# A rewritten beginning, lighter first attention steps, and a halved second group of the first MLP in a hybrid encoder block

## The chip, the cores and the metric

The kernel runs on one core of a Trainium2 chip. The metric is the device time of the whole launch in microseconds (us). A core has a matrix engine (PE, with its weight loads listed apart as PEld), a vector engine (DVE), an activation engine (ACT), a general engine (GpSimd, POOL in the profile) and a sequencer that mainly issues transfers (SP). Each works through its own queue in program order, and waits for others by semaphores.

## The reference

```python
def reference(x, norm1_g, w_in, q_norm_g, k_norm_g, rpb, conv_w, w_attn_branch,
              w_conv_branch, w_o, norm2_g, w_mlp_in, w_mlp_out):
    ...
        u = rms_norm(x, norm1_g[l])
        proj = u @ w_in[l]
        q, k, v, cb, cc, ch, ga, gb = jnp.split(proj, split_pts, axis=-1)
        q = rms_norm(q.reshape(B, S, N_HEADS, HEAD_DIM), q_norm_g[l])
        k = rms_norm(k.reshape(B, S, N_HEADS, HEAD_DIM), k_norm_g[l])
        v = v.reshape(B, S, N_HEADS, HEAD_DIM)
        y_a = neighbourhood_attention(q, k, v, rpb[l]) @ w_attn_branch[l]
        y_b = short_gated_conv(cb, cc, ch, conv_w[l]) @ w_conv_branch[l]
        merged = jax.nn.sigmoid(ga) * y_a + jax.nn.sigmoid(gb) * y_b
        x = x + merged @ w_o[l]
        h = rms_norm(x, norm2_g[l]) @ w_mlp_in[l]
        x = x + jnp.square(jax.nn.relu(h)) @ w_mlp_out[l]
```

There is one layer. x has 1024 tokens of 1024 float32 values, q, k and v are 512 wide (8 heads of 64), the conv's three inputs 512 each, the gates 1024 each, and the MLP's hidden layer 4096. Attention is local on a grid of 16 x 64 tokens, with a relative-position bias.

## The kernel before

**Numbers.** Every float32 operand of a matmul is written as a sum of two float16 tensors, hi (the rounded value, written by ACT or GpSimd) and lo (what is left, written by DVE as `x * scale - hi`). A product then takes three matmuls, hi x hi, hi x lo and lo x hi (`PASSES`). Weight chunks are scaled by a power of two first, which is found from their largest value or their sum of squares: a reduction, a column `ones<-sc`, a matmul with ones (L201) that sums over the partitions, and a few 128x1 operations (`pow2`, `pow2_half`). The scaled chunk's hi pieces are made on ACT (L310), its lo pieces on DVE (L301).

**Tiling.** Tokens are cut into 8 rows of 128. An LN row b goes through the generator `norm`: a square with its sum (ACT L438), the reciprocal root `rstd` (one operation on ACT, five on DVE), the hi half u[b] (GpSimd for rows 1 to 3, ACT otherwise), and the lo half (DVE L446). Then u is transposed to uT: rows 0 to 2 by PE (`ln_trans`, 2 x 8 matmuls with an identity, copied out by ACT and DVE), rows 3 to 7 by a DMA on SP (`ln_turn`). A V unit is 24 matmuls (8 pieces of the inner dimension by three passes). V's weights come as two chunks of 256 columns: units of rows 0 to 2 run as halves (256 wide), those of rows 3 to 7 as one (512 wide). Then follow 8 Q units, 8 K units, and the conv's first chunk.

**Stages.** Begin and V, to 63.6 us; Q, to 105; K, to 148; conv's first part; then attention. In that stage each of the steps k = 0 to 79 issues a score matmul (`at_qk`), a softmax on DVE and ACT (`at_max` L845 is its first operation on DVE), a transposing DMA, and products with V (`at_pv`, L888), and between these `emit(n)` puts conv matmuls. A bias piece for the next quarter is formed in two operations (`bias_make`, DVE L606) at steps 9 and 11 of the 16. Then come the gates and branches, the output projection, and the first MLP from about 650 us. It works in groups (`quad(q)`) of seven products with sums between them; groups 0 and 1 are computed in halves of 256 columns, 0 low, 1 low, 0 high, 1 high. `h_done` then applies relu and square (ACT L1493, L1495), forms sums (L1215, DVE for groups 0 and 1, GpSimd after), and stores the group (`hs<-as`, SP L1506). Behind it comes the second MLP.

**Order.** Nothing is scheduled for the kernel: the order in which Python issues instructions is their order in each engine's queue. Work that runs beside the main line is written as generators: `step()` advances those of the list fg, `tick()` those of bg (weight chunks), `ln_step(b)` the LN row b; a unit's eviction (`post`) goes out after the next unit's matmuls.

`sforms` is one of the fg generators. For a later use (the gates' inputs) it scales pairs of LN rows in place (xt, ACT L499), lets GpSimd form sums and differences of them (L503), and writes these as hi and lo (ACT L508, DVE L510). Its steps are tied to a count of PE units, `SFORM`:

```python
    SFORM = ((6, 0, 0), (7, 1, 0), (8, 0, 1), (10, 2, 0), (10, 1, 1), (11, 3, 0), (14, 2, 1), (15, 3, 1))
        for mark, n, split in SFORM:
            yield from apart(mark, 0)
```

Here (6, 0, 0) is the scaling of rows 0 and 4 when six units are issued, (8, 0, 1) the hi and lo of their sums when eight are.

Of the kernel before, what the change touches and what calls it, by code (L numbers as in the profile page):

```python
# [10 lines left out]
F32 = mybir.dt.float32  # L11
# [41 lines left out]
def encoder_block(ctx: ExitStack, tc: tile.TileContext, x, weights, cols, gqk, rel, masks, out):  # L53
# [12 lines left out]
    def bank(tag):  # L66
        return psum.tile([128, 512], F32, name="ps_" + tag, tag=tag, bufs=banks[tag])
# [132 lines left out]
    def all_sum(a, out, bk, floor, lag=1):  # L200
        T.matmul(bk[:, 0:1], ones[:, 0:128], a, start=True, stop=True)  # L201
# [28 lines left out]
    def load_into(t, ch, p):  # L230
        m = ch.widths[p][0] * ch.widths[p][1]
        SP.dma_start(t, bass.AP(tensor=weights.tensor, offset=weights.offset + ch.offs[p], ap=[[m, 128], [1, m]]))

# [8 lines left out]
    class Chunk:  # L242


        def __init__(self, kind, widths, tag, rows, half, more):
            self.kind, self.bank = kind, {"V": "o", "Q": "o", "K": "s", "C": "d"}.get(kind)
            self.tag, self.rows, self.widths, self.more = tag, rows, widths, more
            self.offs = []
            self.raw, self.ready, self.half = [], more > 0, half
            self.split = False  # L250

        def prep(self):
# [4 lines left out]
            tot = sum(k * w for k, w in self.widths)  # L257
            if self.kind in "QKCG" or self.half:
                self.parts = vhome[0][:, 1] if self.half else wsp.tile([128, 2, tot], F16, name="w16_ws", tag="ws")
# [7 lines left out]
                V.tensor_reduce(sc[:, a], sc[:, at(rm, 0, n)], axis=AX, op=OP.add)  # L267
                c = ones_col()
                V.tensor_tensor(c, sc[:, a], sc[:, gm2], op=OP.mult)
                if self.half:  # L270
                    yield
                else:
                    yield from apart(units[0], 2 if self.kind == "Q" else 3)
                yield from all_sum(c, b, bank(self.bank) if self.bank else anybank(), 1e-36, not self.half)
# [8 lines left out]
            if self.half is not None:  # L283
                if not self.half:
                    vhome.append(wsp.tile([128, 2, 2, tot], F16, name="w16_v", tag="ws"))
                self.parts = vhome[0][:, self.half]
            elif self.kind not in "QKCG":
                self.parts = wpool[self.tag].tile([128, 2, tot], F16, name="w16_" + self.tag, tag=self.tag)
# [27 lines left out]
        def largest(self, rm, a, b):  # L316
# [15 lines left out]
            V.tensor_copy(c, sc[:, a])  # L332
            if self.kind != "V":
                yield from apart(units[0], 3 if self.kind != "O" else 1 + (self is cO[1]))
            yield from all_sum(c, b, bank(self.bank) if self.bank else anybank(), 1e-30, self.kind != "V")

# [97 lines left out]

    def norm(xin, sq, u, y, pool):
# [5 lines left out]
        if pool:  # L441
            G.tensor_scalar(u[:, 0], xin, sc[:, y], 1.0, op0=OP.mult, op1=OP.mult)
        else:
            A.activation(u[:, 0], xin, AF.Copy, scale=sc[:, y])
        yield
        V.scalar_tensor_tensor(u[:, 1], xin, sc[:, y], u[:, 0], op0=OP.mult, op1=OP.subtract)  # L446

    def ln_trans(u16, b, dst):
        for s in range(2):
            pt = bank16("o")  # L450
            for k in range(8):
                T.transpose(pt[:, k * 128:(k + 1) * 128], u16[:, s, k * 128:(k + 1) * 128], ident)
            o = dst[:, s, :, b * 128:(b + 1) * 128]
            i = pt.rearrange("p (k t) -> p k t", k=8)
            if s == 0:
                A.activation(o, i, AF.Copy)
            else:
                V.tensor_copy(o, i)

# [82 lines left out]
    push(cV[0])  # L542
# [8 lines left out]
    ln_step(1, 5)  # L551
    flush()
    v_unit(0, 0, 0, 0)
    ln_step(2)
    push(cV[1])
    tick()
    ln_step(2)
    tick()
    ln_step(1)
    ln_step(2, 5)  # L560
    tick()
    ln_trans(u16[:, 1], 1, UT)
    tick(7)
    v_unit(1, 0, 0, 0)
    ln_step(3)
    ln_step(2)
    tick()
    ln_trans(u16[:, 2], 2, UT)
    ln_step(3)
    tick()  # L570
    ln_step(3, 4)
    fg.append(qk_gain())
    fg.append(sforms())
    for p in range(11):
        if p == 3:
            flush()
            push(cQ)
        if p == 1:
            step()
            tick(2)  # L580
        elif p and p < 6:
            v_unit(p % 3, p // 3, 1, 2)
        elif p > 5:
            v_unit(p - 3, None, 0, 4 if p < 7 else 8)
        for q in (p,) if p < 6 else (2 * p - 6, 2 * p - 5):
            c = q // 2 + 3
            if c < 8 and q % 2 == 0:
                ln_step(c, 2)
                ln_turn(u16[:, c % 4], c, UT)
                turned[0] = c + 1  # L590
            if c < 7:
                ln_step(c + 1, 3)
        if p > 5:
            step(2)
    settle()
# [888 lines left out]
    c1w = c1  # L1484
    bsum, R = [keep(4 if i else 5) for i in range(4)], [(keep(), keep()) for _ in range(4)]
    r_ready = [False] * 4

    def h_done(q, c0=0, c1=512, wait1=0, wait2=0):
# [26 lines left out]
    def quad(q, c0=0, c1=512):  # L1515
# [295 lines left out]
```

## Time and profile before

| | |
|---|---|
| median of 3 runs | 1224.2 us (1222.97 to 1225.59) |
| the profiled execution | 1223.85 us |
| its span, first to last instruction | 1221.9 us |
| PE busy | 1194.5 us, 98%, 6294 matmuls |
| DVE, ACT, POOL busy | 933.2, 763.1, 428.7 us |

The profile is of one execution; its span lies 1.95 us below that execution's time. A row of the timeline has start, duration, engine, line of the kernel, operation, output <- input, shape and count, and in brackets the idle time before it with what ended it. Names are those of the program: w_v and w_ws are the hi and lo weights of V and of Q, K and conv, raw the weights as loaded, u and uT an LN row before and after its transpose, sc small columns of scales, ps_* banks of PSUM, s the forms made by `sforms`, vT the results of V.

### The profile page before, as it was taken

How to read it: one execution, taken by the hardware profiler on the slowest of the kernel's cores; microseconds unless marked ns; L12 is line 12 of the kernel's file. 1: busy time of each engine (PE TensorE's matmuls, PEld its weight loads, DVE VectorE, ACT ScalarE, POOL GpSimd, SP SyncE). 2: the span in 40 equal slices, each digit the busy share in tenths (PEclk: the TensorE clock that was granted, in tenths of full speed). 3: DMA queues.
4: the chain of work that ended last, by engine and by line, in shares of the span. 5: the costliest groups of instructions: out<-in, count | busy, mean ns of one | idle time of the engine just before them, and what ended most of it. 6: DMA issues, size and time to landing. Idle time of an engine off the chain costs nothing.

```text
span 1221.9 us, 17060 instructions
## 1 busy us (share of the span) xinstructions
PE 1194.5 (98%) x6294; PEld 572.8 (47%) x6294; DVE 933.2 (76%) x1754; ACT 763.1 (62%) x1183; POOL 428.7 (35%) x276
## 2 busy tenths in 40 slices
PE   5999999999999999999999999999999999999998
PEld 4544444554444444444458444444444444444444
DVE  6667879888368686887888666456447999998997
ACT  6776678878445455436668777687775754646440
POOL 1430003131321111101004476655658372563562
PEclk9999999999999999999999999999999999999999
DMA  7548556756542121226196455355374935435202
GB/s 278 108 183 180 111 127 123 152 113 131 127 123 61 44 69 40 65 67 244 21 178 173 164 190 163 130 181 175 129 274 164 348 125 183 162 121 207 104 35 104
DMA packets 170867, 173.35 MB, mean 142 GB/s; under 512 B 131488, under 2 KB 132000, under 8 KB 166688
## 3 DMA queue, kind: packets, MB, share of 16 engines
q1 hardware_dynamic: 170208, 168.07, 47.0%
q10 hardware_dynamic: 576, 4.19, 0.9%
q8 instruction: 49, 0.80, 0.3%
q14 instruction: 34, 0.28, 0.1%
HBM read 102.51 MB, written 37.75 MB: 115 GB/s over the span
## 4 chain that ended last, share of the span: by engine, by line
PE 69%; DVE 18%; ACT 7%; issue 4%; DMA 3%; SPq 0%; POOL 0%; ACTq 0%; DVEq 0%
PE ps_d L210 23%; PE ps_s L210 20%; PE ps_o L210 15%; PE ps_d L911 8%; DVE w_s L1033 2%; PE ps_o L888 1%; PE ps_s L831 1%; DVE ops L1644 1%; DMA qD<-q 1%; DVE w L1033 1%; DVE w_ws L301 1%; DVE s L510 1%; DVE sg L1149 1%; ACT w_ws L263 1%; DVE u L446 1%
## 5 line engine op out<-in xcount | busy, mean ns | idle before, releaser
L210 PEld LDWEIGHTS <-ops 128*128 128x128 f16 x1356 | 132.4, 98 | 159.4 <-issue 2.4
L210 PEld LDWEIGHTS <-w 128*128 128x128 f16 x1368 | 132.8, 98 | 141.9 <-issue 2.0
L911 PE MATMUL ps_d<-uT,w_ws 128*128 128x512 f16 x528 | 125.4, 379 | 0.0
L210 PE MATMUL ps_d<-ops 128*128 128x512 f16 (+1 forms) x528 | 118.3, 374 | 0.0
L210 PE MATMUL ps_s<-ops 128*128 128x512 f16 x492 | 113.2, 379 | 1.5 <-DVE sc L112 0.8
L1635 ACT ACTIVATE ops<-hf,sc 128x2048 f16<-128x2048 f32 x26 | 52.0, 1999 | 95.2 <-PE ps_o L210 35.7
L1022 POOL TENSOR_TENSOR tsum<-raw 128x512 f32<-128x512 f32 x28 | 47.2, 1701 | 142.6 <-ACT raw L1008 142.6
L210 PEld LDWEIGHTS <-uT 128*128 128x128 f16 x648 | 63.6, 99 | 68.5 <-issue 5.9
L1215 POOL TENSOR_TENSOR as<-as 128x512 f32<-128x512 f32 x56 | 77.8, 1389 | 43.1 <-ACT as L1495 39.8
L210 PEld LDWEIGHTS <-w_s 128*128 128x128 f16 x588 | 56.7, 98 | 69.5 <-DVE w_s L1033 1.9
L210 PE MATMUL ps_d<-u2x,w 128*128 128x512 f16 (+1 forms) x360 | 80.0, 372 | 0.0
L210 PE MATMUL ps_o<-ops 128*128 128x512 f16 x336 | 77.1, 379 | 0.0
L1637 DVE SCALAR_TENSOR_TENSOR ops<-hf,sc,ops 128x2048 f16<-128x2048 f32 x26 | 72.7, 2795 | 5.2 <-ACT ops L1635 5.2
L911 PEld LDWEIGHTS <-w_ws 128*128 128x128 f16 x528 | 50.8, 98 | 52.5
L210 PE MATMUL ps_o<-u2T,w 128*128 128x512 f16 (+1 forms) x324 | 71.7, 371 | 0.0
L1008 ACT ACTIVATE raw<-raw,sc 128x256 f32<-128x256 f32 x172 | 70.8, 493 | 1.3 <-DMA raw<-in_weights 1.3
L1022 POOL TENSOR_TENSOR gsum<-raw 128x512 f32<-128x512 f32 x14 | 19.0, 1372 | 131.8 <-ACT raw L1008 55.5
L1037 ACT ACTIVATE w<-raw,sc 128x512 f16<-128x512 f32 (+1 forms) x28 | 24.6, 927 | 47.2 <-DVE sc L431 47.2
L210 PE MATMUL ps_s<-u2T,w 128*128 128x512 f16 (+1 forms) x252 | 52.7, 359 | 0.0
L310 ACT ACTIVATE w_ws<-raw,sc 128x512 f16<-128x512 f32 (+2 forms) x72 | 41.0, 636 | 16.1 <-DVE sc L279 16.1
L1528 DVE TENSOR_TENSOR as<-ps_d,as 128x512 f32<-128x512 f32 (+1 forms) x14 | 9.4, 671 | 53.8 <-ACT as L1547 53.8
L854 ACT ACTIVATE sz<-sz,sc 128x384 f32<-128x384 f32 (+1 forms) x64 | 37.2, 581 | 19.6 <-DVE sc L845 12.2
(340 smaller groups left out, 2619.8 us busy)
## 6 DMA issues: line engine op xcount, KB each, us to landing
raw<-in_weights SPq DMA_DIRECT2D x89, 512.0 KB, 5.8
hs<-as SPq DMA_DIRECT2D x16, 1792.0 KB, 8.7
hf<-hs SPq DMA_DIRECT2D x26, 1024.0 KB, 6.2
w2x<-in_weights SPq DMA_DIRECT2D x16, 512.0 KB, 8.1
raw<-in_weights SPq DMA_DIRECT2D x16, 384.0 KB, 3.7
xt<-in_x SPq DMA_DIRECT2D x8, 512.0 KB, 10.1
gs<-s ACTq DMA_DIRECT2D x4, 1024.0 KB, 4.4
x<-in_x SPq DMA_DIRECT2D x8, 512.0 KB, 10.1
```

The costliest lines, as they stand in the source:

```text
L210: T.matmul(ps, l, r, start=a, stop=b)
L263: A.activation(self.parts[:, 1, :k * w].bitcast(BF16), self.raw[p][:, :k * w], AF.Square, accum_out=sc[:, at(rm, p)])
L310: A.activation(self.parts[:, 0, f + o:f + o + m], self.raw[p][:, o:o + m], AF.Copy, scale=sc[:, c:c + 1])
L854: A.activation(z, z, AF.Exp, scale=-1.0, bias=sc[:, d["mx"]], accum_out=sc[:, d["sm"]])
L911: T.matmul(ps, l, r, start=a, stop=b)
L1008: A.activation(v, v, AF.Copy, scale=sc[:, at(g, 4 * i + k)])
L1022: G.tensor_tensor(t[:, o], a, b, op=OP.add)
L1033: V.scalar_tensor_tensor(o(1), w, sc[:, s], o(0), op0=OP.mult, op1=OP.subtract)
L1037: A.activation(o(0), w, AF.Copy, scale=sc[:, s])
L1215: sub.tensor_tensor(z[o], z[a], z[b], op=op)
L1635: A.activation(P[:, 1, 0], hf, AF.Copy, scale=sc[:, Rs])
L1637: V.scalar_tensor_tensor(P[:, 1, 1], hf, sc[:, Rs], P[:, 1, 0], op0=OP.mult, op1=OP.subtract)
```

## The change

It has three parts.

**The begin.** The generators of LN rows 0 to 3 and V's weights are replaced by a list of calls. Row 0's hi half is transposed before V's scale is known, its lo half is made on GpSimd. The scales of rows 1 to 3 are computed on GpSimd (`scale_row`: eight dependent 128x1 operations, one of them a power, then the hi half). V's matmuls of rows 0 to 2 are issued by kinds of partial products: HH and LH first (weights' hi part), HL as the lo weights come. Cols are loaded over ACT's queue, and V's second raw piece as two transfers. After that, LN rows, V units and `step()` are called in another order.

**Attention.** `bias_make` at steps 12 and 14 of the 16 instead of 9 and 11; three conv matmuls instead of four at the end of a step below k = 14 (and at every fourth later), four otherwise, where it was three at all steps but every eighth; a limit for the work beside a step (`SPAN`) of 2150 for 2050.

**First MLP.** Group 1's low half gets its own relu, square and sums (`h_done` on 256 columns), as group 0's already had.

```diff
-    ln = [norm(xt[:, b], sq, u16[:, b % 4], at(ys, b), 0 < b < 4) for b in range(8)]
+    ln = [norm(xt[:, b], sq, u16[:, b % 4], at(ys, b)) for b in range(8)]
...
+    def scale_row(b):
+
+        v, q, y = tmp(), tmp(), at(ys, b)
+        G.tensor_scalar(sc[:, v], sc[:, ss[b]], 4.0 ** -9 / D, 4.0 ** -9 * EPS, op0=OP.mult, op1=OP.add)
+        G.tensor_tensor(sc[:, y], sc[:, v], sc[:, half], op=OP.pow)
+        G.tensor_tensor(sc[:, q], sc[:, y], sc[:, y], op=OP.mult)
+        G.tensor_tensor(sc[:, q], sc[:, q], sc[:, v], op=OP.mult)
+        G.tensor_scalar(sc[:, v], sc[:, q], 0.375, -1.25, op0=OP.mult, op1=OP.add)
+        G.tensor_tensor(sc[:, q], sc[:, q], sc[:, v], op=OP.mult)
+        G.tensor_scalar(sc[:, q], sc[:, q], 1.0, 1.875, op0=OP.mult, op1=OP.add)
+        G.tensor_tensor(sc[:, y], sc[:, y], sc[:, q], op=OP.mult)
+        hi_row(b, G)
...
     ln_step(0, 7)
-    tick()
-    ln_step(1)
-    tick(3)
-    ln_step(0)
-    ln_step(1)
-    tick(4)
-    ln_trans(u16[:, 0], 0, UT)
...
+    lo_row(0, G)
...
+    turn_row(0, 0)()
...
+    v_part(v0, 0, (0,))
+    scale_row(1)
+    v_part(v0, 0, range(1, 8))
+    turn_row(0, 1)()
+    v_part(v0, 1, lower)
+    v_mms(0, 0, range(7), HH, LH)
+    copy = turn_row(1, 0)
+    v_mms(0, 0, (7,), HH, LH)
+    copy()
+    square(2)
+    lo_row(1, V)
...
+    v_part(v1, 0, lower)
+    square(3)
+    scale_row(3)
+    v_part(v1, 0, upper)
+    v_mms(2, 0, eight, HH)
+    turn_row(2, 1)()
+    v_mms(2, 0, eight, HL)
+    v_mms(2, 0, eight, LH)
+    v_post(1, 0, 1)
+    v_part(v1, 1, lower)
+    lo_row(3, V)
+    ln_turn(u16[:, 3], 3, UT)
+    v_part(v1, 1, upper)
+    for ks in lower, upper:
+        for b in range(3):
+            v_mms(b, 1, ks, HH, LH)
+    v_post(2, 0, 0)
+    v_post(2, 0, 1)
+    ln_step(4, 8)
+    ln_turn(u16[:, 0], 4, UT)
...
+    for b in range(3):
+        v_mms(b, 1, eight, HL)
+        if b:
+            v_post(b - 1, 1, 0)
+            v_post(b - 1, 1, 1)
+        step()
+        ln_step(5, 2)
+        tick()
+    for b in range(3, 8):
+        if b == 3:
+            late.append(lambda: (v_post(2, 1, 0), v_post(2, 1, 1)))
+        v_unit(b, 4 if b < 4 else 8)
+        c = b + 2
+        if c < 8:
+            ln_step(c, 2)
+            ln_turn(u16[:, c % 4], c, UT)
+            turned[0] = c + 1
+        if c < 7:
+            ln_step(c + 1, 6)
+        step(2)
...
-        if p < 3 and w in (9, 11):
-            bias_make(*bias[p + 1], (w - 9) // 2)
+        if p < 3 and w in (12, 14):
+            bias_make(*bias[p + 1], (w - 12) // 2)
...
-        emit(4 if k % 8 == 0 else 3)
+        emit(3 if k < 14 or k % 4 == 0 else 4)
...
-            if q == 0:
-                fg.append(h_done(q, c0, c1, 3, 4 if c0 else 24))
-            elif c1 == 512:
-                fg.append(h_done(q, 0, c1, *((2, 6) if q == 1 else (2, 0) if q == 2 else ())))
+            if q < 2:
+                fg.append(h_done(q, c0, c1, *(((3, 24), (3, 4)), ((16, 16), (2, 5)))[q][c0 > 0]))
+            else:
+                fg.append(h_done(q, 0, c1, 2 if q == 2 else 0))
```

How the order changes at three places. First ACT's queue before, from the hi half of LN row 5 (the first u_81; L438 and L412 are a square and its root, L499 `sforms`' scaling, L508 its hi, vT an eviction of V):

```order
L444 ACTIVATE u_81<-xt,sc 128x1024
L438 ACTIVATE sq,sc<-xt 128x1024
L412 ACTIVATE sc<-sc 128x1
L534 ACTIVATE vT<-ps_s 128x256
L499 ACTIVATE xt<-xt,sc 128x1024 x2
L534 ACTIVATE vT<-ps_d 128x256
L444 ACTIVATE u_81<-xt,sc 128x1024
L438 ACTIVATE sq,sc<-xt 128x1024
L412 ACTIVATE sc<-sc 128x1
L499 ACTIVATE xt<-xt,sc 128x1024 x2
L534 ACTIVATE vT<-ps_s 128x512
L444 ACTIVATE u_81<-xt,sc 128x1024
```

And ACT's queue after the change, up to the same hi half of row 5 (the first u_81 here) and on to row 6 (the second); L266 is the sum of squares of a piece of Q's weights, L479 `sforms`' scaling:

```order
L479 ACTIVATE xt<-xt,sc 128x1024 x2
L266 ACTIVATE w_ws,sc<-raw 128x1024
L607 ACTIVATE vT<-ps_d 128x256
L266 ACTIVATE w_ws,sc<-raw 128x1024
L436 ACTIVATE u_81<-xt,sc 128x1024
L433 ACTIVATE sq,sc<-xt 128x1024
L407 ACTIVATE sc<-sc 128x1
L479 ACTIVATE xt<-xt,sc 128x1024 x2
L513 ACTIVATE vT<-ps_s 128x512
L436 ACTIVATE u_81<-xt,sc 128x1024
```

The scaling of rows 0 and 4 stood behind row 5's hi half and now stands ahead of it, and so does that of rows 1 and 5 with row 6.

Second, DVE's queue before, from the lo half of row 7 to the second lo of `sforms` (L510); L301 are the lo pieces of Q's weights, and an eviction and the scale's steps (L204 to L279) are left out between the two parts:

```order
L446 SCALAR_TENSOR_TENSOR u_81<-xt,sc,u_81 128x1024
L510 TENSOR_TENSOR s_559<-xt,s_559 128x4x512
L535 SCALAR_TENSOR_TENSOR vT<-ps_d,vT 128x512
```

```order
L301 SCALAR_TENSOR_TENSOR w_ws<-raw,sc,w_ws 128x512 x2
L535 SCALAR_TENSOR_TENSOR vT<-ps_s,vT 128x512
L301 SCALAR_TENSOR_TENSOR w_ws<-raw,sc,w_ws 128x512 x6
L510 TENSOR_TENSOR s_653<-xt,s_653 128x4x512
```

And after the change (L490 is the lo of `sforms`, L438 the lo half of row 7, L297 the lo pieces of Q's weights), with an eviction and the same steps of the scale left out:

```order
L490 TENSOR_TENSOR s_565<-xt,s_565 128x4x512
L514 SCALAR_TENSOR_TENSOR vT<-ps_d,vT 128x512
L438 SCALAR_TENSOR_TENSOR u_81<-xt,sc,u_81 128x1024
```

```order
L297 SCALAR_TENSOR_TENSOR w_ws<-raw,sc,w_ws 128x512 x2
L490 TENSOR_TENSOR s_648<-xt,s_648 128x4x512
L514 SCALAR_TENSOR_TENSOR vT<-ps_d,vT 128x512
L297 SCALAR_TENSOR_TENSOR w_ws<-raw,sc,w_ws 128x512 x6
```

Each lo of `sforms` has moved ahead of the work that it stood behind: the first ahead of row 7's lo half, the second ahead of the last six lo pieces.

Third, DVE's queue in the first MLP before, at group 1's sums (L1215), behind the scale's steps (L204 to L432) and an eviction (L1549):

```order
L204 TENSOR_SCALAR sc<-ps_s 128x1
L425 TENSOR_SCALAR sc<-sc 128x1
L427 TENSOR_SCALAR sc<-sc 128x1
L429 TENSOR_SCALAR sc<-sc 128x1
L431 TENSOR_SCALAR sc<-sc 128x1
L432 TENSOR_SCALAR sc<-sc 128x1
L1549 TENSOR_TENSOR as<-ps_o,t_5801 128x512
L1215 TENSOR_TENSOR as<-as 128x512 x4
```

And after:

```order
L1333 TENSOR_TENSOR as<-as 128x256 x4
L204 TENSOR_SCALAR sc<-ps_s 128x1
L1333 TENSOR_TENSOR as<-as 128x256 x4
L420 TENSOR_SCALAR sc<-sc 128x1
L422 TENSOR_SCALAR sc<-sc 128x1
L424 TENSOR_SCALAR sc<-sc 128x1
L426 TENSOR_SCALAR sc<-sc 128x1
L427 TENSOR_SCALAR sc<-sc 128x1
L1667 TENSOR_TENSOR as<-ps_o,t_5812 128x512
```

The four sums of 512 columns have become two times four of 256, and stand ahead of the scale's steps and the eviction.

More of the change, by code (lines that the diff above doesn't have):

```diff
@@ L282, in prep @@
                 yield WAIT
[L283 to L287, printed above, removed]
+            if self.kind not in "QKCG":
                 self.parts = wpool[self.tag].tile([128, 2, tot], F16, name="w16_" + self.tag, tag=self.tag)
@@ L440, in norm @@
         yield from rstd(ss, D, y, 9)
[L441 to L444, printed above, removed]
+        A.activation(u[:, 0], xin, AF.Copy, scale=sc[:, y])
         yield
         V.scalar_tensor_tensor(u[:, 1], xin, sc[:, y], u[:, 0], op0=OP.mult, op1=OP.subtract)
[L448 to L458, printed above, removed]
     def ln_turn(u16, b, dst):
@@ new lines, in v_sum, with v_scale, v_part @@
+    def v_sum(ch, c):
+        ch.sum = bank("o")
+        T.matmul(ch.sum[:, 0:1], ones[:, 0:128], c, start=True, stop=True)
+    def v_scale(ch, floor, power):
+        V.tensor_scalar(sc[:, ch.b], ch.sum[:, 0:1], floor, None, op0=OP.max)
+        for _ in power:
+            pass
+        V.tensor_scalar(sc[:, ch.rm], sc[:, g1], sc[:, ch.s], None, op0=OP.mult)
+    def v_part(ch, s, ks):
+        for k in ks:
+            p, o = k // 4, k % 4 * 256
+            hi, lo = (ch.parts[:, w, k * 256:(k + 1) * 256] for w in range(2))
+            raw, c = ch.raw[p][:, o:o + 256], sc[:, at(ch.rm, k)]
+            if s == 0:
+                A.activation(hi, raw, AF.Copy, scale=c)
+            else:
+                V.scalar_tensor_tensor(lo, raw, c, hi, op0=OP.mult, op1=OP.subtract)
+                if k % 4 == 3:
+                    done[0] += 1
+                    load_upto(done[0] + 5)
@@ L540, in encoder_block @@
+    HH, HL, LH = PASSES
+    ss, half, lower, upper, eight = {}, tmp(), range(4), range(4, 8), range(8)
+    G.memset(sc[:, half], -0.5)
     V.tensor_reduce(sc[:, gm2], sc[:, g1], axis=AX, op=OP.max, apply_absolute_value=True)
     mul(gm2, gm2, gm2)
-    push(cV[0])
-    ln_step(0, 7)
-    tick()
-    ln_step(1)
-    tick(3)
-    ln_step(0)
-    ln_step(1)
-    tick(4)
-    ln_trans(u16[:, 0], 0, UT)
[L551 to L556, printed above, removed]
@@ new lines, in encoder_block @@
+    copy()
+    square(2)
+    lo_row(1, V)
+    v_part(v0, 1, (4, 5))
+    v_mms(0, 0, lower, HL)
+    turn_row(1, 1)()
+    v_part(v0, 1, (6, 7))
+    scale_row(2)
+    for p in range(2):
+        A.activation(v1.parts[:, 1, 1024 * p:1024 * p + 1024].bitcast(BF16), v1.raw[p], AF.Square,
+                     accum_out=sc[:, at(v1.rm, p)])
+    v_mms(1, 0, eight, HH)
+    v_mms(0, 0, (4, 5), HL)
+    v_mms(1, 0, eight, LH)
+    v_mms(0, 0, (6, 7), HL)
+    v_mms(1, 0, eight, HL)
+    V.tensor_reduce(sc[:, v1.a], sc[:, at(v1.rm, 0, 2)], axis=AX, op=OP.add)
@@ L572, in encoder_block @@
+    lo_row(3, V)
[8 more added lines that the diff above has]
+    ln_turn(u16[:, 0], 4, UT)
+    turned[0] = 5
     fg.append(qk_gain())
     fg.append(sforms())
[L574 to L594, printed above, removed]
+    push(cQ)
@@ L1484, in encoder_block @@
     c1w = c1
[L1485 removed]
+    bsum, R = [keep(4 if i else 6) for i in range(4)], [(keep(), keep()) for _ in range(4)]
     r_ready = [False] * 4
```

132 lines of the change are left out of this document (93 added, 39 removed).

## The prediction

> **What bounds the kernel now.** I read the page's first part, then PE's waits over the whole span, and then the timeline of the three places that the diff touches.
>
> ```profile
> PE 1194.5 (98%) x6294; PEld 572.8 (47%) x6294; DVE 933.2 (76%) x1754; ACT 763.1 (62%) x1183; POOL 428.7 (35%) x276
> PE ps_o L201 <- DVE ones L332: 10.3, 1, 10.3
> PE ps_s L831 <- DVE sc L845: 3.0, 5, 1.2
> PE ps_d L210 <- DVE w_v L301: 2.7, 2, 1.7
> PE ps_s L201 <- DVE ones L989: 1.7, 1, 1.7
> PE ps_d L210 <- DVE w_ws L301: 0.9, 2, 0.5
> ```
>
> PE is busy 98% and the number of matmuls does not change, so only PE's idle time can move: 1221.9 - 1194.5 = 27.4 us. The five rows of waits (us in all, times, longest) name the stages: 10.3 before the first matmul and 2.7 for V's lo weights in the begin, 3.0 in the first attention steps, 1.7 in the first MLP, 0.9 at K's first unit. The last two parts of the change can win 3.0 and 1.7 at most. The begin can win more, and since PE works there in the order in which LN rows and weights come, it can also lose more.
>
> **The begin.** Units of PE from the timeline (start, duration):
>
> ```profile
> 10.33 1.01 PE L452 MATMUL ps_o<-ident,u 128*128 128x128 f16 x8
> 37.58 5.34 PE L210 MATMUL ps_s<-w_v,uT 128*128 128x512 f16 x24
> 42.76 5.34 PE L210 MATMUL ps_d<-w_v,uT 128*128 128x512 f16 x24
> 47.97 5.34 PE L210 MATMUL ps_s<-w_v,uT 128*128 128x512 f16 x24
> 58.38 5.35 PE L210 MATMUL ps_s<-w_v,uT 128*128 128x512 f16 x24
> 63.57 5.34 PE L210 MATMUL ps_d<-w_ws,uT 128*128 128x512 f16 x24
> 68.75 3.62 PE L210 MATMUL ps_o<-w_ws,uT 128*128 128x512 f16 x16
> ```
>
> V's row 3 starts at 37.58, and from there to Q's second unit at 68.75 a unit follows every 5.18 to 5.2 us: PE waits for nothing, and what the begin wins before 37.58 is kept only if LN rows 5, 6 and 7 come earlier by as much. They have no room: the transpose of row 7 goes out after its lo half, and lands just before 58.38. So I walked the new order of each queue, with durations from these rows:
>
> ```profile
> 14.15 1.59 POOL L442 TENSOR_SCALAR u<-xt,sc 128x1024 f16<-128x1024 f32 x1 [13.09 <-DVE sc L420]
> 20.00 1.12 POOL L442 TENSOR_SCALAR u<-xt,sc 128x1024 f16<-128x1024 f32 x1 [4.26 <-DVE sc L267]
> 28.59 1.28 DVE L446 SCALAR_TENSOR_TENSOR u<-xt,sc,u 128x1024 f16<-128x1024 f32 x1 [1.25 <-POOL u L442]
> 30.41 1.66 DVE L301 SCALAR_TENSOR_TENSOR w_v<-raw,sc,w_v 128x256 f16<-128x256 f32 x4
> 32.57 1.15 ACT L444 ACTIVATE u<-xt,sc 128x1024 f16<-128x1024 f32 x1 [2.12 <-DVE sc L420]
> 40.22 1.13 ACT L444 ACTIVATE u<-xt,sc 128x1024 f16<-128x1024 f32 x1
> 43.14 2.18 ACT L499 ACTIVATE xt<-xt,sc 128x1024 f32<-128x1024 f32 x2
> 51.80 1.91 ACT L508 ACTIVATE s<-xt 128x2048 f16<-128x2048 f32 x1
> 51.87 2.21 DVE L446 SCALAR_TENSOR_TENSOR u<-xt,sc,u 128x1024 f16<-128x1024 f32 x1 [0.35 <-ACT u L444]
> 54.01 3.35 DVE L510 TENSOR_TENSOR s<-xt,s 128x2048 f16<-128x2048 f32 x1
> 63.57 4.05 DVE L301 SCALAR_TENSOR_TENSOR w_ws<-raw,sc,w_ws 128x512 f16<-128x512 f32 x6
> uT<-u SPq DMA_TRANSPOSE x5, 4.2
> 0.34 0.10 POOL L1802 MEMSET const-uint8-127<- 128x1 uint8 x1
> 0.83 0.23 POOL L392 IOTA idi<- 128x128 int32 x1 [0.39 <-POOLq L1802]
> ```
>
> GpSimd's eight small operations of a row's scale, the power among them, stand nowhere in this trace. The nearest rows are a 128x1 memset of 0.10 and the iota of 0.23; I take 0.2 each, 1.6 us a row, nearer to the upper row because each waits for the one before it.
>
> - *Start.* Row 0 is transposed as soon as its hi half is there, about 8.0 where it was 10.33, with the lo half on GpSimd (a scaling of 1.12, and a subtraction of about 1.4) beside the search for V's largest weight. Cols on ACT's queue and the halved load are issue slots of 0.4 us that save at most 0.3; I count them in this.
> - *Rows 1 to 3.* Hi halves end near 13.9 (before 14.15 + 1.59 = 15.7), 20.1 (before 21.1), and 28.3 (before 28.6, where DVE goes on). Row 3 gains next to nothing: its square stands behind four pieces of V's second half on ACT, and these behind V's second scale at 22.7. DVE waits for GpSimd here, runs row 3's lo half 28.3 to 29.6, then four more lo pieces (1.66) and row 4's scale: row 4's hi half starts at 32.7, as before (32.57).
> - *V.* Kinds of partial products let PE fill its waits: rows 0 to 2 are done near 33.5, row 3's transposes land at 29.6 + 4.3 = 33.9, and V's row 3 starts at 34.0: -3.6.
> - *Row 5.* Between hi 4 and hi 5 ACT had 40.22 - 32.57 = 7.65 us of work without a gap. The new order puts the two scalings of xt (2.18) and one more eviction (0.37) ahead of hi 5, so it starts 10.3 us after 32.7, at 43.1. Lo 5, issue and landing add 1.15 + 1.3 + 4.3: V's row 5 can start at 49.9, not 47.97. The gain is gone and PE stands 5 us.
> - *Rows 6 and 7.* The second pair of scalings comes ahead of hi 6, the first s (1.91) ahead of hi 7, and on DVE its lo half (3.35) ahead of lo 7, which ends at 58.3. The transpose lands at 62.6: V's row 7 at 62.65 instead of 58.38, Q's first unit at 67.8.
> - *Q's weights.* The second s is now formed between the two halves of Q's hi weights on ACT (2.18 + 1.91) and ahead of six lo pieces on DVE (about 3.0). These end near 74.6, so Q's first unit stalls 2 us inside, and the second starts at 75.2 instead of 68.75: **+6.4**.
>
> Bounds: with 0.1 a small operation the walk gives about +5.5, with 0.3 +8.5. If row 4's scale did not stand behind GpSimd, hi 4 would come at 30 and the end at +3.8. One nearer +8 follows if lo halves take 2.21, as the one beside GpSimd's subtractions did, instead of 1.28.
>
> The Trainium skill's GPSIMD Engine Reference (section 3.1) gives DVE's dispatch as about 156 ns and says that GpSimd has two software hops where DVE has one. Taken as an estimate of twice 156 ns, a small operation would be 0.31 and the begin +8.7; the trace's memset and iota are below it, so the sum stays with 0.2.
>
> **What of that is absorbed.** The q and k vectors lag behind PE:
>
> ```profile
> 76.14 0.67 ACT L612 ACTIVATE qs<-ps_d,sc 128x512 f32<-128x512 f32 x1
> 105.05 0.38 PE L210 MATMUL ps_d<-w_ws,uT 128*128 128x512 f16 x1
> 111.72 0.59 PE L210 MATMUL ps_o<-w_ws,uT 128*128 128x512 f16 x2
> 164.49 0.48 DVE L845 CUSTOM_DVE_ANT_0 sz<-ps_s,bias,sc 128x256 f32<-128x256 f32 x1 [3.01 <-DMA kD<-k]
> ```
>
> Q's first result was done at 68.9 and read at 76.14, and K's first unit took 111.72 - 105.05 = 6.67, that is 1.5 more than 5.18, because its lo weights stood behind that work on DVE. A PE that comes 6 us later finds them ready: **-1.5**. Behind K, where the vectors catch up with PE, the rest travels on into attention.
>
> **Attention.** The steps near 180 to 190 held two bias operations (the first is shown); now they come three steps later.
>
> ```profile
> 179.60 0.61 DVE L606 SCALAR_TENSOR_TENSOR bias<-bias,sc,mk 128x384 f32<-128x384 f32 x1
> 187.13 1.90 DVE L301 SCALAR_TENSOR_TENSOR w_ws<-raw,sc,w_ws 128x384 f16<-128x384 f32 x2
> 189.62 0.38 PE L831 MATMUL ps_s<-kD,qD 128*128 128x256 f16 x2 [1.21 <-DVE sc L845]
> ```
>
> That takes 2 x 0.61 from DVE ahead of the steps that wait 3.0 in all. It can win 1.8 of these at most, since the longest wait, 1.21, is behind a weight pair of 1.90 that stays; it can win nothing, because fewer conv matmuls a step (7 for 7.125) leave PE less beside the softmax. I take **-0.9**, the middle. At the end of attention conv runs out some four steps earlier, so the last three products with V stand without cover: **+0.3** (0 to 1).
>
> **First MLP.** The chain of its 1.7 us:
>
> ```profile
> 683.37 2.86 DVE L1215 TENSOR_TENSOR as<-as 128x512 f32<-128x512 f32 x4
> 686.29 0.53 SPq L1506 DMA_DIRECT2D hs<-as  x1
> 695.03 0.60 ACT L1547 ACTIVATE as<-ps_o 128x512 f32<-128x512 f32 x1 [4.65 <-DMA hs<-as]
> 701.52 4.05 DVE L1033 SCALAR_TENSOR_TENSOR w<-raw,sc,w 128x512 f16<-128x512 f32 x2
> 721.53 2.20 DVE L1033 SCALAR_TENSOR_TENSOR w<-raw,sc,w 128x512 f16<-128x512 f32 x2
> 718.11 0.16 PE L201 MATMUL ps_s<-ones 128*128 128x1 bf16 x1 [1.69 <-DVE ones L989]
> ```
>
> The store of group 1 goes out at 686.29, after the four sums. ACT's next eviction needs that buffer and waits 4.65; everything after it on DVE falls among GpSimd's additions, where a weight pair takes 4.05 instead of 2.20, until PE waits 1.69. With halves, half of the squares is done from 665 on, and the sums stand around the scale's first operation near 680: the store goes out about 4 us earlier, most of the 4.65. **-1.7** (0 to -1.7).
>
> **Sum.** +6.4 - 1.5 - 0.9 + 0.3 - 1.7 = +2.6. The profiled execution was 1223.85 (span 1221.9), 0.35 below the median of 1224.2; on the median this is **1226.8**. Its own range, from begins of +3.8 and +8.5 with the other terms as they stand, is 1224.2 to 1228.9. What a measurement of this kernel can tell from no change is 0.2%, 2.4 us.
>
> **Rivals.**
> - *As meant: the LN rows come in time.* If GpSimd makes row 4's scale much earlier, and hi 5 with it, then -3.6 stays. The 2.55 us more ahead of hi 5 on a full ACT speak against it. It gives -3.6 - 0.9 + 0.3 - 1.7 = -5.9, 1218.3; if the vectors do not come earlier too, K's wait grows and about 1221 is left. Chance 0.17.
> - *The later PE finds no waits.* If the q and k vectors do not shift with PE at all (they lag 7 us at Q's first, and DVE has 3.01 idle for kD's landing), the later PE meets none of the attention's waits, 3.0 rather than 0.9: 6.4 - 1.5 - 3.0 + 0.3 - 1.7 = +0.5, 1224.7, or 1222.1 with the walk's lower end, and under 1221.7 where a part of kD's landing is absorbed too. Against it: Q's lo weights on DVE, hence the vectors behind them, come later as well. Chance 0.2.
> - *GpSimd's small operations are dear.* At 0.4 to 0.5 each, or a power of a microsecond or more, rows 1 and 3 and all behind them come 2 to 8 us later than in the sum: 1229 to 1235. It decides from 0.3 on. No row of the trace excludes it. Chance 0.15.
> - *A first call that loads code.* A wait of 6 us before GpSimd's first power would delay row 1's hi half, and with V's later rows behind it the end by up to as much: 1232.8. The first scaling on GpSimd at 14.15 took 1.59 where a later one took 1.12, so a first call shows half a microsecond at most. Chance 0.05. The Trainium skill's GPSIMD Engine Reference (section 2.1, Instruction dispatch) says that a freshly loaded kernel's first call pays about 6 us that no profiled instruction shows; by that rule this rival would hold, and the trace at 14.15 does not agree for scalings, while no run here shows a power.
>
> The sum above has the other 0.43, of it 0.20 within 0.2% and 0.23 slower. From the cases: faster 0.17 + 0.05 = 0.22; within 0.2% 0.15 + 0.20 = 0.35; slower 0.23 + 0.15 + 0.05 = 0.43. The range 1218 to 1231 leaves out the best of the first rival, the worse half of the third, and the fourth.
>
> **What would show it.** Right: V's row 3 near 34 but an idle PE of some 5 us before V's row 5 and again before row 7, with uT as releaser; Q's second unit near 75; K's first unit without its 1.5; ACT's 4.65 wait near 695 and PE's 1.69 gone; a DVE wait for GpSimd before row 3's lo half. Wrong: V's rows 3 to 7 at steps of 5.2 from 34, or GpSimd's small operations far from 0.2. The step on which most rests is hi 5's start at 43.1: if it comes at 40, the forecast falls by 3 us.

## The result and the profile after

The change made the kernel slower: median 1234.64 us of 6 runs (1234.12 to 1236.13) against 1224.05 us of 6 runs before; ratio 1.0087, 95% interval 1.0077 to 1.0098, that is 10.6 us. The forecast was 1226.8, with a range of 1218 to 1231: the sign was right, the size four times too small, and the time lies above the range.

The profiled execution of the changed kernel took 1236.13 us, the longest of its six, span 1234.4. Its page, and PE's longest waits (us in all, times, longest):

```profile
PE 1199.6 (97%) x6294; PEld 575.3 (47%) x6294; DVE 933.4 (76%) x1743; ACT 764.4 (62%) x1183; POOL 435.4 (35%) x303
PE ps_o L554 <- ACT u L436: 9.0, 1, 9.0
PE ps_d L210 <- DVE w_ws L297: 5.7, 6, 1.4
PE ps_s L210 <- DMA uT<-u: 3.9, 2, 3.1
PE ps_s L949 <- DVE sc L963: 2.2, 2, 1.6
PE ps_o L554 <- POOL u L526: 1.8, 1, 1.8
PE ps_o L570 <- DVE ones L630: 1.6, 1, 1.6
PE ps_d L210 <- DMA uT<-u: 1.5, 1, 1.5
```

PE's first wait is 1.3 us shorter than before, and the MLP's (1.7 on the ones column) is gone. New are the waits for Q's lo weights (5.7, six times) and for the transposes of LN rows (3.9 and 1.5). PE's units in the begin (start, duration):

```profile
39.50 5.34 PE L210 MATMUL ps_s<-w_v,uT 128*128 128x512 f16 x24
46.37 5.35 PE L210 MATMUL ps_d<-w_v,uT 128*128 128x512 f16 x24 [1.52 <-DMA uT<-u]
54.86 7.04 PE L210 MATMUL ps_s<-w_v,uT 128*128 128x512 f16 x24 [3.14 <-DMA uT<-u]
61.77 5.34 PE L210 MATMUL ps_d<-w_v,uT 128*128 128x512 f16 x24
67.90 5.35 PE L210 MATMUL ps_s<-w_v,uT 128*128 128x512 f16 x24 [0.79 <-DMA uT<-u]
73.09 1.67 PE L210 MATMUL ps_d<-w_ws,uT 128*128 128x512 f16 x7
76.13 0.81 PE L210 MATMUL ps_d<-w_ws,uT 128*128 128x512 f16 x3 [1.37 <-DVE w_ws L297]
...
84.94 5.34 PE L210 MATMUL ps_o<-w_ws,uT 128*128 128x512 f16 x24
```

V's row 3 starts 1.9 us later than before (39.50 for 37.58), V's row 7 9.5 later (67.90 for 58.38), and Q's second unit 16.2 later (84.94 for 68.75). The last 6.7 us of this come inside Q's first unit, which takes 11.85 instead of 5.18: it creeps along behind six lo pieces on DVE. Of the 16.2 us 12.3 are left at the end of the two profiled executions (1236.13 for 1223.85): K's first unit gives 1.5 back and the MLP 1.7. The 0.7 that are left I do not place for certain; PE's waits in attention are 0.8 shorter than before (2.2 for 3.0). What DVE and GpSimd do at that time:

```profile
67.38 2.17 ACT L479 ACTIVATE xt<-xt,sc 128x1024 f32<-128x1024 f32 x2
69.63 14.28 POOL L483 TENSOR_TENSOR xt<-xt 128x512 f32<-128x512 f32 x8 [10.45 <-ACT xt L479]
71.39 3.02 DVE L490 TENSOR_TENSOR s<-xt,s 128x2048 f16<-128x2048 f32 x1 [4.30 <-ACT s L488]
74.93 9.53 DVE L297 SCALAR_TENSOR_TENSOR w_ws<-raw,sc,w_ws 128x512 f16<-128x512 f32 x6
```

The six pieces are the same six that took 4.05 in the kernel before (L301 there, at 63.57). There they were done when GpSimd began its second batch of `sforms`' sums and differences, in the kernel before:

```profile
65.28 2.18 ACT L499 ACTIVATE xt<-xt,sc 128x1024 f32<-128x1024 f32 x2
67.53 12.52 POOL L503 TENSOR_TENSOR xt<-xt 128x512 f32<-128x512 f32 x8 [7.71 <-ACT xt L499]
```

In the changed kernel they lie inside that batch, and each takes 1.59 instead of 0.68.

### The profile page after: what moved, and what is told of

Same layout as the page of the kernel before. It is cut to its first block, busy times and chain, and to the rows that moved or that the text cites. A ratio compares the mean times of both kernels' runs of the same rounds, so it can differ in the third digit from the quotient of the medians.

```text
span 1234.4 us, 17077 instructions
## 1 busy us (share of the span) xinstructions
PE 1199.6 (97%) x6294; PEld 575.3 (47%) x6294; DVE 933.4 (76%) x1743; ACT 764.4 (62%) x1183; POOL 435.4 (35%) x303
## 4 chain that ended last, share of the span: by engine, by line
PE 40%; DVE 5%; ACT 2%; issue 2%; DMA 1%; DVEq 0%; ACTq 0%
PE ps_d L210 16%; PE ps_s L210 13%; PE ps_o L210 11%; DVE ops L1762 1%; DMA u2T<-v 1%; DVE form L1333 1%; DVE v L1381 1%; ACT as L1611 0%; DMA u2x<-v 0%; DVE ops L1755 0%; DVE w L1151 0%; DVE x L1516 0%; ACT ops L1753 0%; ACT u2x L1341 0%; ACT ops L1721 0%
## 5 line engine op out<-in xcount | busy, mean ns | idle before, releaser
L210 PEld LDWEIGHTS <-uT 128*128 128x128 f16 x504 | 49.2, 99 | 73.1 <-issue 9.6
L297 DVE SCALAR_TENSOR_TENSOR w_ws<-raw,sc,w_ws 128x512 f16<-128x512 f32 (+2 forms) x72 | 50.7, 756 | 4.0 <-ACT w_ws L306 4.0
## 6 DMA issues: line engine op xcount, KB each, us to landing
x<-in_x SPq DMA_DIRECT2D x8, 512.0 KB, 10.2
```

The costliest lines, as they stand in the source:

```text
L210: T.matmul(ps, l, r, start=a, stop=b)
L297: V.scalar_tensor_tensor(lo, self.raw[p][:, o:o + m], sc[:, c:c + 1], hi, op0=OP.mult, op1=OP.subtract)
```

## The experiments

Three theories for the 10.6 us: *order* (the place of `sforms`' work, ahead of LN rows' hi halves on ACT and ahead of Q's lo pieces on DVE and beside GpSimd); *GpSimd* (the rows' scales computed there are slow, and everything starts late); and the two other parts of the change losing something too. All times are medians; the kernel before, on the same chips, was 1223.6 to 1224.0.

**The parts.** The begin alone (changed kernel, attention and MLP as before), then the attention part alone and the MLP part alone on the kernel before:

```diff
 e1: after, with
-    SPAN = 2150
+    SPAN = 2050
 ... (bias_make, emit and h_done as before)
 e2: before, with
+    SPAN = 2150
+        if p < 3 and w in (12, 14):
+        emit(3 if k < 14 or k % 4 == 0 else 4)
 e3: before, with
+                fg.append(h_done(q, c0, c1, *(((3, 24), (3, 4)), ((16, 16), (2, 5)))[q][c0 > 0]))
```

> The changed kernel with attention and first MLP put back as before: the begin alone. By the traces Q's second unit starts 16.2 us later (84.94 for 68.75). If the loss is the begin's alone and the other two parts win what the trace after shows (1.86 at 718, nothing in attention), this is slower than the whole change by 1 to 2 us: 1235.5 to 1236.5. If attention or the MLP lose (the wait at 665.62 grew from 0.5 to 1.1), it is faster than the whole change: 1232 to 1234.

> Before, with only the attention part. My forecast's term: -0.9 (0.2 to -1.8). Rival, from the trace after, where the same waits stand 10 us later with the same sum (3.7 per 50 us in both): 0.0, within 0.5.

> Before, with only the MLP part. If the 1.7 us wait at 718 goes and nothing takes its place: -1.7 us, 1222.3. If the wait at the first stored group (665.62 in the trace after, 1.1 for 0.5) belongs to this part: -1.1, 1222.9.

Measured: the begin alone 1237.03 (ratio 1.0108, 1.0094 to 1.0121), that is +13.4; attention alone 1223.86 (1.0002, 0.9993 to 1.0011), nothing; MLP alone 1221.95 (0.9984, 0.9975 to 0.9993), -1.7. So the loss is the begin's. (The three sum to 11.9 against the change's 10.6, which lies within their intervals.)

**Forms later.** In the changed kernel each of the first six marks of `sforms` one later:

```diff
-    SFORM = ((6, 0, 0), (7, 1, 0), (8, 0, 1), (10, 2, 0), (10, 1, 1), (11, 3, 0), (14, 2, 1), (15, 3, 1))
+    SFORM = ((7, 0, 0), (8, 1, 0), (9, 0, 1), (11, 2, 0), (11, 1, 1), (12, 3, 0), (14, 2, 1), (15, 3, 1))
```

> The changed kernel with sforms' marks one later, so that the scalings of xt stand behind the hi halves of rows 5 and 6 and its second lo behind Q's lo pieces, as before. Theory 'order' (the forms' place makes the loss): Q's six lo pieces fall from 9.53 to about 4.1, hi 5 comes 2.5 earlier; Q's second unit at 76 to 78, the time 1227 to 1229. Theory 'GpSimd' (the rows' scales are late from the start): hi 4 stays at 37.8, V's row 5 waits as before within 2.5 us, and the time falls by 3 us at most, to 1231.5 or more.

Measured 1224.49 (1.0007, 0.9997 to 1.0016): 10.1 us less than the change, more than theory *order* had asked for (1227 to 1229). In its trace:

```profile
35.99 1.15 ACT L436 ACTIVATE u<-xt,sc 128x1024 f16<-128x1024 f32 x1 [0.87 <-DVE sc L415]
43.74 1.15 ACT L436 ACTIVATE u<-xt,sc 128x1024 f16<-128x1024 f32 x1
62.84 5.35 PE L210 MATMUL ps_s<-w_v,uT 128*128 128x512 f16 x24 [0.79 <-DMA uT<-u]
73.21 5.34 PE L210 MATMUL ps_o<-w_ws,uT 128*128 128x512 f16 x24
67.22 4.06 DVE L297 SCALAR_TENSOR_TENSOR w_ws<-raw,sc,w_ws 128x512 f16<-128x512 f32 x6
71.19 12.53 POOL L483 TENSOR_TENSOR xt<-xt 128x512 f32<-128x512 f32 x8 [8.26 <-ACT xt L479]
```

The lo pieces are through before GpSimd begins, and take 4.06; Q's second unit starts at 73.21. The hi half of row 4 (35.99) stays late.

**Which of the forms.** Only the first three marks later (the first pair of scalings and s), and only the later three (second scaling, s and its lo):

```diff
 e5
+    SFORM = ((7, 0, 0), (8, 1, 0), (9, 0, 1), (10, 2, 0), (10, 1, 1), (11, 3, 0), (14, 2, 1), (15, 3, 1))
 e6
+    SFORM = ((6, 0, 0), (7, 1, 0), (8, 0, 1), (11, 2, 0), (11, 1, 1), (12, 3, 0), (14, 2, 1), (15, 3, 1))
```

> The changed kernel with only the first three marks of sforms one later (scalings behind hi 5 and hi 6, first lo behind lo 7); the second s and its lo stay ahead of Q's six lo pieces. Theory 'two causes': V's rows 5 to 7 come in time (row 7 near 63 instead of 67.9), but Q's lo pieces still take 9.5: Q's second unit near 80, time 1229 to 1231. If Q's lo pieces fall to 4.1 here too, the second cause is not their place: 1225.

> The changed kernel with only the last marks one later (second s and its lo behind Q's lo pieces). Theory 'two causes': V's rows 5 to 7 wait as in the change (row 7 at 67 to 68), Q's lo pieces take 4.1, Q's second unit at 78 to 79: time 1228 to 1230. Rival (the LN rows decide all of it): no gain, 1234.

Measured: e5 1234.93, no gain at all where 1229 to 1231 was expected; e6 1227.63, 7.0 faster than the change and a little better than expected (its six lo pieces take 4.05). In e5 V's row 7 came at 62.73, 5 us earlier than in the change, and none of it was left when Q's first unit was done:

```profile
67.92 1.67 PE L210 MATMUL ps_d<-w_ws,uT 128*128 128x512 f16 x7
74.60 1.44 PE L210 MATMUL ps_d<-w_ws,uT 128*128 128x512 f16 x3 [5.01 <-DVE w_ws L297]
...
83.40 5.34 PE L210 MATMUL ps_o<-w_ws,uT 128*128 128x512 f16 x24
```

PE now waits 5.01 us for the third lo piece. The two losses stand one behind the other, and the second hides the first: the first forms' place costs 3.1 (e6 against e4) only when the second's is mended.

**Contention or place.** The change with GpSimd's eight later operations cut to one column (most of these sums are then left out; all positions stay); and the kernel before with the second pair's marks moved, once all of it, once only the scaling, after which s and lo stay behind Q's lo pieces:

```diff
 e9: after, with
-                    G.tensor_tensor(z[o], z[a], z[b], op=op)
+                    m = 512 if n < 2 else 1
+                    G.tensor_tensor(z[o][:, :m], z[a][:, :m], z[b][:, :m], op=op)
 e11: before, with
-    ... (10, 2, 0), (10, 1, 1) ...
+    ... (9, 2, 0), (9, 1, 1) ...
 e12: before, with
+    ... (9, 2, 0), (10, 1, 1) ...
```

> The changed kernel with sforms' eight later operations on GpSimd (pairs 2/6 and 3/7) cut to one column each, which leaves most of these sums and differences out. All positions in the queues stay. Theory 'GpSimd beside DVE': Q's six lo pieces take 4.1 instead of 9.5, Q's second unit starts near 79.5, time about 1230 (the rest is the s ahead of them and the late rows). Rival (the place in DVE's queue is what costs): they stay at 9.5 and the time at 1234.

> The kernel before with sforms' marks of the second pair at 9 instead of 10, which puts its scaling, its s and its lo ahead of Q's last hi and lo pieces, as in the change; nothing else. Theory: Q's six lo pieces 9.5, Q's second unit 8 to 11 us later, time 1230 to 1232. If the loss needs the changed begin, it stays within 2 us of 1223.6.

> The kernel before with only the second pair's scaling at 9, s and lo stay behind Q's lo pieces: GpSimd's subtractions then run beside DVE's lo pieces, with the same order on DVE as before. Theory 'GpSimd beside DVE': lo pieces take up to 9.5, Q's second unit 4 to 5.5 us later, time 1226 to 1228. Theory 'place in the queue': no change, 1223.6.

Measured: e9 1227.66 (-7.0 against the change, more than expected); e11 1233.90 (1.0083, 1.0070 to 1.0097), above the 1230 to 1232 expected; e12 1227.04 (1.0025, 1.0014 to 1.0037), as expected. The six lo pieces, first in e9, then in e11, then in e12:

```profile
72.91 4.06 DVE L297 SCALAR_TENSOR_TENSOR w_ws<-raw,sc,w_ws 128x512 f16<-128x512 f32 x6
```

```profile
70.42 9.53 DVE L301 SCALAR_TENSOR_TENSOR w_ws<-raw,sc,w_ws 128x512 f16<-128x512 f32 x6
65.14 14.26 POOL L503 TENSOR_TENSOR xt<-xt 128x512 f32<-128x512 f32 x8 [4.78 <-ACT xt L499]
```

```profile
66.11 8.15 DVE L301 SCALAR_TENSOR_TENSOR w_ws<-raw,sc,w_ws 128x512 f16<-128x512 f32 x6
65.06 6.30 POOL L503 TENSOR_TENSOR xt<-xt 128x512 f32<-128x512 f32 x4 [4.77 <-ACT xt L499]
```

So it is contention: take GpSimd's work away and the same pieces at the same place take 4.06; put it beside them with DVE's order untouched (e12) and they take 8.15. And it needs nothing of the new begin: two marks moved from 10 to 9 make the old kernel 10 us slower. In the changed kernel the contention is, as far as these times tell, the whole of the second loss: e9, which leaves every position as it is, ends at 1227.66, and e6, which moves the work, at 1227.63. In the kernel before, where V's rows are in time, the place counts too: the second s and its lo ahead of the pieces add most of the rest (e11 against e12, 6.9 us, of which 1.4 is the longer contention, 9.53 for 8.15).

**GpSimd's scales, and V's scale.** All forms later as in e4; then with rows' scales on DVE and ACT, or with V's second sum ahead of row 2's transposes on PE:

```diff
 e7: as e4, with
-        G.tensor_tensor(sc[:, y], sc[:, v], sc[:, half], op=OP.pow)
- ... (the eight operations of scale_row)
+        for _ in rstd(ss[b], D, at(ys, b), 9):
+            pass
 e8: as e4, with
-    copy = turn_row(2, 0)
     v_sum(v1, c)
+    copy = turn_row(2, 0)
```

> All marks of sforms later (as e4, 1224.5), and the scales of rows 1 to 3 on DVE and ACT (six operations a row) instead of GpSimd; hi halves stay on GpSimd. Theory 'GpSimd is dear' (its operations take 0.3 on average, 3 us a row with their gaps, where before had 2.5): hi 4 a microsecond or two earlier than 36, time 1222.5 to 1224. Rival: the place of the operations does not matter, since DVE's queue is as late: 1224.5 within 0.7.

> As e4, with the matmul that sums V's second chunk ahead of row 2's transposes on PE's queue, which wait for GpSimd's hi half. Theory: V's second scale, hence hi pieces, row 3's square and hi 4, come about 1.5 us earlier than in e4; time 1223 to 1224. Rival: row 2's own lateness decides: no change from 1224.5.

Measured 1224.55 and 1224.39, against 1224.49 of e4: no difference in either, both rivals right. In e8 DVE still formed V's scale behind row 2's lo half, which waits for GpSimd. The next two runs put that right, and then LN row 4 ahead as well; e14 is e13 without the attention part:

```diff
 e10: as e4, with
-    copy = turn_row(2, 0)
     v_sum(v1, c)
-    copy()
-    lo_row(2, V)
     v_scale(v1, 1e-36, pow2_half(v1.b, 14, v1.s, v1.inv, v1.more))
+    v_post(0, 0, 0)
+    v_part(v1, 0, lower)
+    copy = turn_row(2, 0)
+    copy()
+    lo_row(2, V)
 ... (square(3) right behind V's sums of squares)
 e13: as e10, with
+    ln_step(4, 1)
+    turn_row(2, 1)()
     v_mms(2, 0, eight, HH)
 ... (row 4's scale and hi half behind lo_row(3, V))
```

> As e4 (1224.5), with V's second scale ahead of everything that waits for row 2's hi half, on PE (sum), DVE (scale before lo 2) and ACT (hi pieces before the copy), and row 3's square before it. Theory (hi 4's 36 instead of 32.6 is what is left): hi 4 at 32 to 33.5, V's rows 3.4 us earlier, time 1221.5 to 1222.5. Rival (the row's scale by GpSimd keeps it): hi 4 at 35 or more, 1224.

> As e10 (1222.7), with LN row 4 ahead: its square and scale stand ahead of V's second lo pieces and evictions, and row 2's lo transposes ahead of its first matmuls, on which DVE waited 3.89 in e10. Theory (row 4's lateness is the whole rest of the begin's loss, since rows 5 to 7 follow it in steps of 5.2 to 7.8): hi 4 at 30 to 32, Q's second unit at 67.5 to 70, time 1220 to 1221.5. Rival (the vectors behind Q give a gain back as the wait at K's first unit): Q's second unit earlier as said, but the time stays within 0.7 of e10's.

> As e13, with the attention part put back as before. If the attention part is worth nothing (e2: +0.2): the same within 0.7. If it pays only when PE is early or late there, as e1 and the whole change suggest (1237.0 against 1234.6 with the MLP's 1.7 between them): 0.7 to 1.8 slower than e13.

Measured: e10 1222.67 (0.9993, 0.9984 to 1.0001), row 4's hi half at 35.26 and not at 32 to 33.5. That is 0.7 earlier than in e4, and Q's second unit (72.49) comes 0.7 earlier too, so the larger part of its gain over e4 (0.0014 in the ratios, 1.7 us) did not come by the step expected and has no cause shown; e13 1220.96 (0.9977, 0.9968 to 0.9986), e14 1220.96 (0.9980, 0.9971 to 0.9989). In e13:

```profile
31.72 1.15 ACT L436 ACTIVATE u<-xt,sc 128x1024 f16<-128x1024 f32 x1 [3.32 <-DVE sc L415]
69.54 5.34 PE L210 MATMUL ps_o<-w_ws,uT 128*128 128x512 f16 x24
105.83 5.34 PE L210 MATMUL ps_d<-w_ws,uT 128*128 128x512 f16 x24
111.00 1.24 PE L210 MATMUL ps_o<-w_ws,uT 128*128 128x512 f16 x5
```

e13 beats both kernels: 2.65 us faster than before, 13.7 faster than the change. Its MLP part accounts for 1.7 (e3). Its begin is no shorter than the old one (Q's second unit at 69.54 for 68.75); K's first unit, at 105.83, runs its 5.2 us where the old kernel lost 1.5.

## Why the prediction was wrong

**A part of the frame was right.** The loss is the begin's and comes from `sforms`' place on ACT and DVE, which the order alone had shown. e4 confirms it: with the marks one later, the 10 us go. Two parts were wrong. The walk had V's row 3 at 34.0, a gain of 3.6 us that LN row 5 then loses; it started at 39.50 in the change, 37.39 in e4 and 37.58 before, so there was no gain to lose. And not only PE's idle time moved: its busy time grew from 1194.5 to 1199.6 us with the same 6294 matmuls, because PE ran at half clock in two stretches: the granted clock was 0.74 from 20 to 30 us, 0.92 from 30 to 40 and 0.83 from 50 to 60, which makes the 5.1 (the last section has rows).

**The step that failed is "Q's weights", +6.4.** It priced the six lo pieces at 4.05, from a row of the kernel before in which GpSimd was idle, and so had Q's first unit end at 75.2. They took 9.53 beside GpSimd: 5.5 of the 9.7 us by which Q's second unit (84.94) missed the forecast (75.2). The prediction had noticed the same effect one step earlier, on the LN lo halves (2.21 instead of 1.28 beside the same subtractions), and used it as a bound there; it did not ask what GpSimd would be doing when the lo pieces ran. Moving the scaling on ACT moved the releaser of GpSimd's second batch from behind these pieces to ahead of them. The walk gave this batch no place at all. That this step failed is shown by e9: without the batch the pieces take 4.06, at the same place.

**The other 4.2 us are the start.** The walk had row 4's hi half at 32.7, and it came at 37.82. Rows, with GpSimd's operations of row 1 first and V's largest weight beside row 0's lo half:

```profile
9.12 2.12 POOL L535 TENSOR_TENSOR u<-f,u 128x1024 f16<-128x1024 f32 x1
10.14 1.13 DVE L102 TENSOR_TENSOR sc<-sc 128x8 f32<-128x8 f32 x1
12.25 0.19 POOL L540 TENSOR_SCALAR sc<-sc 128x1 f32<-128x1 f32 x1 [1.00 <-ACT sq L520]
12.53 0.56 POOL L541 TENSOR_TENSOR sc<-sc 128x1 f32<-128x1 f32 x1
...
15.20 1.23 POOL L526 TENSOR_SCALAR u<-xt,sc 128x1024 f16<-128x1024 f32 x1
23.89 1.28 DVE L531 SCALAR_TENSOR_TENSOR u<-xt,sc,u 128x1024 f16<-128x1024 f32 x1 [1.60 <-POOL u L526]
26.02 0.23 DVE L576 TENSOR_SCALAR sc<-sc 128x8 f32<-128x8 f32 x1
33.45 1.29 DVE L531 SCALAR_TENSOR_TENSOR u<-xt,sc,u 128x1024 f16<-128x1024 f32 x1 [2.42 <-POOL u L526]
37.82 1.15 ACT L436 ACTIVATE u<-xt,sc 128x1024 f16<-128x1024 f32 x1 [0.87 <-DVE sc L415]
```

The eight operations of row 1 take 15.20 - 12.25 = 2.95 us, 0.37 each and not 0.2. The Trainium skill's GPSIMD Engine Reference (section 3.1), which counts two software hops for GpSimd against DVE's one, had led to an estimate of 0.31; the trace stands nearer to that than to my 0.2.

This is a term mis-sized by itself. Rows 2 and 3 take 2.82 and 3.11 us where the walk had 1.6, PE waits 1.81 for row 2's hi half and DVE 2.42 for row 3's. By these figures up to 1.2 + 1.5 = 2.7 of the 5.1 us are theirs, which is an estimate. They get in through the queues behind: V's second scale stood behind row 2's hi half on PE and on DVE and came at 26.02, not 22.7, and row 3's square, row 4's square and row 4's scale behind it. e7 does not price the operations alone: there row 3's hi half starts 1.2 earlier than in e4 (29.24 for 30.45), but DVE, which now computes the scales too, comes to row 3's lo half no sooner (31.74 for 31.61). e13 shows that the order can take them off the path, with row 4's hi half at 31.72.

Smaller terms: an 8-column product on DVE took 1.13 instead of 0.17 while GpSimd subtracted row 0's lo half. And 1.8 of the 5.1 belong to this execution: in e4, whose queues are the same up to there, row 4's hi half started at 35.99. Of that, 0.9 is the first row of x, which landed later (row 0's hi half at 7.83, in e4 at 6.95).

**The terms that held.** From row 4's hi half to row 5's the walk had 10.3 (its terms, 7.65 + 2.18 + 0.37, give 10.2), and it took 9.85 (37.82 to 47.67). K's first unit no longer loses its 1.5. The MLP's -1.7 was measured alone as -1.7, and by the step forecast: in e3 the store goes out at 682.46 for 686.29, and ACT's next eviction (692.22) no longer waits. The attention's -0.9 was not found in the time: the bias operations left, and the waits fell from 3.0 to 2.2 in all (the longest, behind the weight pair of 1.90, grew from 1.2 to 1.6), but alone the part measured +0.2, with an interval of about 1 us each way, and e13 and e14 are equal. Where the 0.8 goes is open.

**The rivals.** The first (as meant) needed LN rows in time, which they were not. The second, a later PE that meets no waits, holds for K but not for the attention. The third, dear operations on GpSimd, had nearly its condition (0.37 for 0.4), and its 1229 to 1235 holds the measured time, but by luck: e4 keeps all these operations and is 10.1 us faster than the change. The fourth, a first call that loads code, did not occur: the first power on GpSimd (L541 above) started 0.28 after the operation before it began and took 0.56. The Trainium skill's GPSIMD Engine Reference (section 2.1, Instruction dispatch) gives about 6 us for the first call of a freshly loaded kernel; this trace shows none of it.

## What to carry to other kernels

A duration can depend on what runs beside it, as DVE's lo pieces did here (1.59 for 0.68) and ACT's hi pieces did not: before a price from the old trace is put into a new order, ask what the other engines will be doing at the new time, above all an engine that the moved instruction releases. Where two waits stand one behind the other, mending the first alone shows nothing (e5), so a null result for one part is no verdict on it until the second is out of the way. A generator that runs beside the main line is moved by any change in the number of calls between its marks: look at where its instructions land, not only at those that were rewritten.

## What the runs showed of the hardware

**GpSimd beside DVE.** Lo pieces with two tensors as inputs took 0.68 alone and 1.59 beside GpSimd's additions, and these 1.78 each (14.28 for 8) where the first batch took 1.54 each (6.17 for 4, at 53.01). The lo of `sforms` (128x2048, two tensors as inputs) took 3.02 beside them and 2.29 in e9 without them. ACT's hi pieces in the same stretch took 2.55 for four in the changed kernel and 2.54 before. The Trainium skill's GPSIMD Engine Reference (section 1, Specifications) says that GpSimd shares its memory interfaces with VectorE, and that DVE's instructions with two inputs in SBUF contend; these rows agree, and put a factor of 2.3 on it.

**PE's clock fell after waits.** The unit at 54.86 took 7.04 where all others take 5.34 or 5.35. Its stretches, and ahead of them one from an earlier dip, with the granted clock in the column behind POOL's:

```profile
28.00:30.00 2.00, 2.00 (x13) 1.50 (x12) 1.58 (x4) 2.00 (x6) 0.74 (x2) 0.50 0.00 0
52.00:54.00 2.00, 0.00 (x0) 0.00 (x0) 1.01 (x5) 2.00 (x3) 0.99 (x1) 1.00 1.15 212
54.00:56.00 2.00, 1.14 (x5) 0.53 (x6) 1.65 (x2) 1.50 (x3) 1.84 (x3) 0.90 0.15 28
56.00:58.00 2.00, 2.00 (x6) 0.64 (x5) 1.66 (x5) 1.19 (x2) 1.92 (x2) 0.50 0.02 5
58.00:60.00 2.00, 2.00 (x8) 0.85 (x7) 1.97 (x3) 2.00 (x3) 1.18 (x1) 0.75 1.15 216
```

After 3.14 us without work PE ran at half clock for some 3.4 us, and the unit took 1.7 us more. The kernel did not: V's row 7 still waits 0.79 for its transpose, and starts 30.1 us after row 4's hi half, as it does in e1 without this dip (30.2). The earlier dip, from about 24.5 to 31 us (24 matmuls of 256 columns took 4.50, in e4 2.87), followed two waits of 1.81 and 1.11, after which e4's clock stayed at 1.00. The same unit took 7.04 in e6 and e9, after idle times of 3.91 and 3.56, but 5.35 in e1, after 3.77. The Trainium skill's TensorE: Matmul & The Clock Gate (Part 1) speaks of an idle window of about 3.4 us that runs free of the program; that would explain why the longer idle time in e1 went unpunished, but no run here shows the window itself, and the trace does not agree in full, since the 3.14 us and the two waits at 22 to 26 us are shorter than such a window. In the kernel before no wait behind the first matmul reached 2 us, and the granted clock stayed at 1.00. A long wait on PE can thus lengthen the unit behind it; whether the kernel pays for it depends on the next wait.
